# All dense products of a hybrid decoder layer by Strassen's seven block products, with attention and recurrence fed from DRAM

## The chip, the core and the metric

The kernel runs on one core of a Trainium2 chip. Its engines are TensorE (PE: matrix products, with PEld its weight loads), VectorE (DVE), ScalarE (ACT), GpSimd (POOL) and SyncE (SP, which here only issues DMAs). Each works through its own list of instructions in order and waits at semaphores for the others. The metric is the device time of one execution in microseconds (us). TensorE's clock has two levels, 1.2 and 2.4 GHz; the profile gives the granted clock as a share of the higher.

## The reference, cut to what matters

One layer over x of 2048 tokens by 1024 features, all in float32:

```
h = x @ w_in                       # (2048,1024) @ (1024,3328)
hq, hf, hi, hg, aq, ak, av, ag = split(h)   # 512,512,512,512 | 512,128,128,512
f   = lb + (1-lb) * sigmoid(hf);  k_in = 1 - f;  q_h = silu(hq)
o_h = hgrn2_chunk(q_h, k_in, hi, log f)     # 4 heads of 128, state 128x128, chunks
o_h = rmsnorm(o_h) * hg_norm_w * silu(hg)
o_a = sliding_window_attention(rope(aq), rope(ak), av, sinks) * silu(ag)
      # 8 query heads and 2 key/value heads of 64, window 128
out = concat(o_h, o_a) @ w_out     # (2048,1024) @ (1024,1024)
z   = 2**0.25 * x + out
return layernorm(z) * ln_g + ln_b
```

The recurrence is S_t = diag(f_t) S_(t-1) + (1-f_t) i_t^T with output S_t^T q_t.

## The kernel before, in words

Every dense product is made with operands split in two: a rounded part `h` (ACT, line 97) and the remainder `l` (line 98, on DVE, or for two of the four x tiles of a block on POOL). Three matmuls, h·h, h·l and l·h, replace one float32 product. `load_split` (line 87) loads a tile from DRAM by SP and splits it. `project_t` (line 104) makes one 128 x 512 product of a weight tile and 512 tokens: eight K tiles, 24 matmuls of 128x512, lines 110 to 112. `project_n` (line 114) does the same with tokens on the partitions, lines 120 to 122.

Three stages follow one another. Attention goes over two key/value heads `j` and four blocks `b` of 512 tokens: it loads and splits x, projects (`kvp`, `qp`, `gp`), rotates, makes scores `sp`, weights `wt`, and the mix, which goes to DRAM (`sw_spill`, line 329). The recurrence goes over two pairs of heads and the same four blocks, loads x again, projects decay and query (`fp`, `hq`), and per 128 tokens values and gates (`vg`); two chunks of 128 tokens then share small products: scores `ap` (lines 444, 447), transposed keys `kp` (line 454) copied by ACT to `kt` (line 459), state updates `hkv` (line 475), outputs `ho` (lines 488, 492), whose squares ACT sums (line 495). The result goes to `hg_spill` (line 506). The output stage takes 16 tiles of 128 tokens: `prepare` (line 333) loads the mix, transposes half of it (`mp`, line 342) and splits it; 48 matmuls give two halves `po` (lines 537 to 539), DVE adds the residual (`z`, line 540) and the layer norm follows.

The program's text is not the order on an engine: a scheduler of the framework moves each instruction as early as its list allows, and the pools set when a buffer is free again: `mm`, `sc` (three accumulators each), `rawp` (3), `wp` (8), `xp` (7). Sixteen matmuls on zeros (line 128) run while the first loads are under way.

## Time and profile before

| | |
|---|---|
| time, median of 3 runs | 949.61 us (949.59 to 952.05) |
| profiled execution: span | 951.3 us |
| PE busy | 933.0 us (98%) |
| PE weight loads busy | 750.7 us (79%) |
| DVE busy | 607.3 us (64%) |
| ACT busy | 308.4 us (32%) |
| POOL busy | 322.0 us (34%) |
| moved by DMA | 91.03 MB, mean 96 GB/s |

The profiled execution is one run with the profiler on; its span from first to last instruction is 951.3 us, 0.18% above the median of the timed runs. Busy times of matmuls overlap, since one enters the array while the one before drains; the step from one matmul to the next is read from a chain instead.

### The profile page before, as it was taken

What the parts mean: (1) busy time and instruction counts of PE and PEld (TensorE: products, weight loads), DVE (VectorE), ACT (ScalarE), POOL (GpSimd) and SP (SyncE); (2) the same over time, 40 slices, a digit from 0 to 9 for tenths busy, and PEclk for the clock granted to TensorE, in tenths of its full rate; (3) what the DMA queues carried; (4) which work ended last, traced back from release to release, by engine and by line L of the source; (5) the groups of instructions that cost most, each with busy time, mean ns of one, the idle gap of its engine ahead of it and who ended that gap; (6) DMA issues with size and microseconds to landing.
All of it is one profiled execution on the core that took longest, in us unless ns stands there. A gap on an engine that the chain in (4) does not pass through costs nothing.

```text
span 951.3 us, 12917 instructions
## 1 busy us (share of the span) xinstructions
PE 933.0 (98%) x4744; PEld 750.7 (79%) x4744; DVE 607.3 (64%) x1233; ACT 308.4 (32%) x785; POOL 322.0 (34%) x306
## 2 busy tenths in 40 slices
PE   8999999999998999999999999999999989999996
PEld 7878777777786777878887887888788878888885
DVE  5877887867879955726366383726458446666554
ACT  5455545544564423131142423122133211000000
POOL 1645536445447534313042642313133111111111
PEclk9999999999999999999999999999999999999998
DMA  7423243033242403002032321103013253444321
GB/s 261 165 72 123 70 158 124 33 106 106 78 151 94 127 12 101 23 12 100 1 122 78 100 100 65 47 1 102 10 56 123 78 188 134 143 152 146 113 99 57
DMA packets 33216, 91.03 MB, mean 96 GB/s; under 512 B 4224, under 2 KB 12416, under 8 KB 33152
## 3 DMA queue, kind: packets, MB, share of 16 engines
q1 hardware_dynamic: 27792, 73.41, 23.7%
q0 software_dynamic: 2912, 8.40, 2.5%
q10 hardware_dynamic: 2448, 8.39, 2.2%
q8 instruction: 37, 0.61, 0.3%
q14 instruction: 27, 0.22, 0.1%
HBM read 73.41 MB, written 16.78 MB: 95 GB/s over the span
## 4 chain that ended last, share of the span: by engine, by line
PE 85%; DVE 6%; DMA 4%; ACT 3%; issue 1%; SPq 0%; POOL 0%; POOLq 0%; DVEq 0%; ACTq 0%
PE vg L121 6%; PE vg L120 6%; PE vg L122 6%; PE po L537 6%; PE po L539 6%; PE po L538 6%; PE fp L110 3%; PE fp L111 3%; PE fp L112 3%; PE hq L112 3%; PE hq L110 3%; PE hq L111 3%; PE op L320 3%; PE qp L112 2%; PE qp L110 2%; PE qp L111 2%
## 5 line engine op out<-in xcount | busy, mean ns | idle before, releaser
L537 PE MATMUL po<-wo_h,mh 128*128 128x512 f32 (+1 forms) x264 | 103.1, 391 | 2.8 <-DVE z L540 2.8
L539 PE MATMUL po<-wo_h,ml 128*128 128x512 f32 (+1 forms) x264 | 102.0, 386 | 0.0
L538 PE MATMUL po<-wo_l,mh 128*128 128x512 f32 (+1 forms) x264 | 101.9, 386 | 0.0
L120 PE MATMUL vg<-wh_h,xh_h 128*128 128x512 f32 x256 | 100.8, 394 | 0.0
L121 PE MATMUL vg<-wh_l,xh_h 128*128 128x512 f32 x256 | 100.8, 394 | 0.0
L122 PE MATMUL vg<-wh_h,xh_l 128*128 128x512 f32 x256 | 100.7, 394 | 0.0
L98 POOL TENSOR_TENSOR xh_l<-xh_raw,xh_h 128x1024 fp32r<-128x1024 f32 x16 | 39.1, 2448 | 125.6 <-ACT xh_h L97 122.9
L540 DVE SCALAR_TENSOR_TENSOR z<-xr,po 128x512 f32<-128x512 f32 (+1 forms) x33 | 22.1, 672 | 70.3 <-PE po L539 64.3
L545 POOL TENSOR_SCALAR rs<-mv 128x1 f32<-128x1 f32 x16 | 9.4, 584 | 151.4 <-DVE mv L543 151.4
L283 ACT ACTIVATE wt<-sp,st 128x128 f32<-128x128 f32 x128 | 45.8, 365 | 44.4 <-DVE st L279 44.0
L537 PEld LDWEIGHTS po<-wo_h,mh 128*128 128x128 f32 x264 | 50.1, 190 | 12.4 <-DVE z L540 3.0
L293 POOL TENSOR_TENSOR wt<-wt,st 128x512 f32<-128x512 f32 x32 | 37.4, 1169 | 61.9 <-DVE st L292 35.2
L539 PEld LDWEIGHTS po<-wo_h,ml 128*128 128x128 f32 x264 | 50.0, 189 | 10.1
L538 PEld LDWEIGHTS po<-wo_l,mh 128*128 128x128 f32 x264 | 50.0, 189 | 9.5
L343 ACT ACTIVATE mh<-mp 128x512 fp32r<-128x512 f32 x16 | 9.6, 599 | 144.8 <-PE mp L342 144.8
L120 PEld LDWEIGHTS vg<-wh_h,xh_h 128*128 128x128 f32 x256 | 48.4, 189 | 10.1 <-issue 0.6
L121 PEld LDWEIGHTS vg<-wh_l,xh_h 128*128 128x128 f32 x256 | 48.1, 188 | 10.2 <-issue 0.6
L122 PEld LDWEIGHTS vg<-wh_h,xh_l 128*128 128x128 f32 x256 | 48.1, 188 | 9.9 <-issue 0.4
L395 DVE RECIPROCAL re<-e 128x512 f32<-128x512 f32 x16 | 53.5, 3344 | 0.0
L433 DVE SCALAR_TENSOR_TENSOR hg<-tg,vg 128x256 f32<-128x256 f32 x32 | 13.4, 420 | 60.2 <-ACT tg L431 60.2
L110 PE MATMUL fp<-xh_h,wh_h 128*128 128x512 f32 x128 | 51.2, 400 | 0.0
L110 PE MATMUL qp<-xa_h,wa_h 128*128 128x512 f32 x128 | 50.7, 396 | 0.0
(173 smaller groups left out, 2483.9 us busy)
## 6 DMA issues: line engine op xcount, KB each, us to landing
xh_raw<-in_xt_dram SPq DMA_DIRECT2D x32, 512.0 KB, 3.6
xa_raw<-in_xt_dram SPq DMA_DIRECT2D x28, 512.0 KB, 3.7
wh_raw<-in_wt_dram SPq DMA_DIRECT2D x16, 512.0 KB, 3.4
xr<-in_xn_dram SPq DMA_DIRECT2D x16, 512.0 KB, 3.6
out_dram<-y ACTq DMA_DIRECT2D x15, 512.0 KB, 2.6
wa_raw<-in_wt_dram SPq DMA_DIRECT2D x9, 512.0 KB, 4.9
cs<-in_rope_dram SPq DMA_DIRECT2D x8, 512.0 KB, 3.4
sw_spill<-mix POOLq DMA_DIRECT2D x32, 128.0 KB, 2.5
```

Of the source, the lines that this page charges most:

```text
L98: engines[lo_eng].tensor_sub(lo[:, c], raw[:, c], hi[:, c].bitcast(F32))
L110: nc.tensor.matmul(ps, lhsT=wh[:, r], rhs=xh[:, c], start=k == 0, stop=False)
L111: nc.tensor.matmul(ps, lhsT=wh[:, r], rhs=xl[:, c], start=False, stop=False)
L112: nc.tensor.matmul(ps, lhsT=wl[:, r], rhs=xh[:, c], start=False, stop=k == KT - 1)
L120: nc.tensor.matmul(ps, lhsT=xh[:, r], rhs=wh[:, c], start=k == 0, stop=False)
L121: nc.tensor.matmul(ps, lhsT=xh[:, r], rhs=wl[:, c], start=False, stop=False)
L122: nc.tensor.matmul(ps, lhsT=xl[:, r], rhs=wh[:, c], start=False, stop=k == KT - 1)
L283: nc.scalar.activation(wt_[:, s, :], sps[s // 2][:, s % 2, P:], AF.Exp, bias=st[:, 1, s : s + 1], scale=0.125, accum_out=st[:, 3, s : s + 1],)
L395: nc.vector.reciprocal(re, e[:, :, 1:129])
L537: nc.tensor.matmul(ps, lhsT=mh[:, e, :], rhs=wh[:, c], start=e == 0, stop=False)
L538: nc.tensor.matmul(ps, lhsT=mh[:, e, :], rhs=wl[:, c], start=False, stop=False)
L539: nc.tensor.matmul(ps, lhsT=ml[:, e, :], rhs=wh[:, c], start=False, stop=e == 7)
```

## The change

The kernel is written anew around 2 x 2 block products in Strassen's manner (the variant with seven products and shared sums). x is taken in two super-blocks `s` of 1024 tokens. In each, x is cut in halves by tokens and by K into `a11`, `a12`, `a21`, `a22`, and the seven operands `a11`, `a12`, `a22`, `s1` to `s4` are made by DVE, split (`put`), and kept on chip for the super-block, one buffer each. The 26 weight tiles are taken in 13 pairs; the seven combinations of a pair's blocks are made and split (`w_rest`), four of them go to DRAM in the first super-block (`kept_w`) and are loaded again in the second. A product is four K tiles of three matmuls. `Pair` runs the seven into accumulators `px`, `py`, `pz`; ACT takes three snapshots of them, DVE adds three times, and four 128 x 512 projections come out, which `finish` writes to DRAM: queries, keys and values of attention split (`hl`), the rest whole (`proj`). For the first three pairs of a super-block, the products 1 and 2 of all three stand ahead of the others (GROUP).

Attention (`attend`) and recurrence (`recur`) load from DRAM what they need. A table `jobs` says ahead of which pair each of the eight attention and eight recurrence blocks is written; two recurrence blocks come in the output stage. The recurrence loads its values and gates transposed and turns them by PE (128 transposes of 128 x 128, line 540 after). The output product takes pairs of token tiles: seven operands of w_out take the x operands' buffers, and seven of each mixed pair are made by DVE and POOL. Accumulators are six in one pool. The POOL DMA queue's scratch is 4096 bytes.

```diff
-LO_ENGINES = "dpdp"
+PAIRS = [(0, 5), (1, 2), (3, 4), (6, 7), (8, 9)] + [
+    (10 + 8 * j + 2 * i, 11 + 8 * j + 2 * i) for j in range(2) for i in range(4)
+]
+GROUP = 3
...
+    def split2(src, h, l):
+        nc.scalar.activation(h, src, AF.Copy)
+        nc.vector.tensor_sub(l, src, h.bitcast(F32))
+    def w_split(src, name):
+        w = w_tile(name)
+        split2(src, w[:, 0], w[:, 1])
+        return w
+    def put(made, n, q, src, name):
+        h = xc.tile([P, 512], F32R, tag=f"{n}{q}h", name=f"{name}_{n}{q}h")
+        l = xc.tile([P, 512], F32R, tag=f"{n}{q}l", name=f"{name}_{n}{q}l")
+        split2(src, h, l)
+        made[n][q] = (h, l)
...
+    def x_sums(s, made):
+        n = f"x{s}"
+        for q in range(4):
+            a21, a22 = load_x(s, 1, q, f"{n}_p21{q}"), load_x(s, 1, 4 + q, f"{n}_p22{q}")
+            a11 = load_x(s, 0, q, f"{n}_p11{q}")
+            s1, s2 = tmp_tile(f"{n}_s1{q}"), tmp_tile(f"{n}_s2{q}")
+            nc.vector.tensor_add(s1, a21, a22)
+            nc.vector.tensor_sub(s2, s1, a11)
+            put(made, "s2", q, s2, n)
+            put(made, "s1", q, s1, n)
+        for q in range(4):
+            a11, a21 = load_x(s, 0, q, f"{n}_r11{q}"), load_x(s, 1, q, f"{n}_r21{q}")
+            s3 = tmp_tile(f"{n}_s3{q}")
+            nc.vector.tensor_sub(s3, a11, a21)
+            put(made, "s3", q, s3, n)
+        for q in range(4):
+            a12 = load_x(s, 0, 4 + q, f"{n}_r12{q}")
+            s4 = tmp_tile(f"{n}_s4{q}")
+            h, l = made["s2"][q]
+            nc.vector.tensor_sub(s4, a12, h.bitcast(F32))
+            nc.vector.tensor_sub(s4, s4, l.bitcast(F32))
+            put(made, "s4", q, s4, n)
+        for q in range(4):
+            put(made, "a22", q, load_x(s, 1, 4 + q, f"{n}_r22{q}"), n)
...
+    def w_rest(s, pair, w, again):
+        n = f"w{s}_{pair[0]}"
+        if s == 1:
+            for m in (6, 5, 7):
+                w[m] = w_tile(f"{n}_{m}")
+                nc.sync.dma_start(w[m].bitcast(F32), kept_w[pair, m])
+            w[3] = w_split(load_w(s, pair[1], 1, ""), f"{n}_3")
+            w[4] = w_tile(f"{n}_4")
+            nc.sync.dma_start(w[4].bitcast(F32), kept_w[pair, 4])
+            return
+        b11, b21 = load_w(s, pair[0], 0, ""), load_w(s, pair[0], 1, "")
+        b12, b22 = load_w(s, pair[1], 0, ""), load_w(s, pair[1], 1, "")
+        if not again:
+            w[1], w[2] = w_split(b11, f"{n}_1"), w_split(b21, f"{n}_2")
+        def keep(m, t):
+            w[m] = w_split(t, f"{n}_{m}")
+            nc.gpsimd.dma_start(kept_w[pair, m], w[m].bitcast(F32))
+        t1, t2 = tmp_tile(f"{n}_t1"), tmp_tile(f"{n}_t2")
+        nc.vector.tensor_sub(t1, b12, b11)
+        nc.vector.tensor_sub(t2, b22, t1)
+        keep(6, t2)
+        keep(5, t1)
+        nc.vector.tensor_sub(t1, b22, b12)
+        keep(7, t1)
+        w[3] = w_split(b22, f"{n}_3")
+        nc.gpsimd.tensor_sub(t2, b21, t2)
+        keep(4, t2)
...
+    def finish(pair, row, col, s, t):
+        w, b = pair[col], 2 * s + row
+        if w >= 10:
+            nc.gpsimd.dma_start(proj[w][b], t)
+            return
...
+        h, l = t_tile(f"h{w}_{b}", F32R), t_tile(f"l{w}_{b}", F32R)
+        split2(t, h, l)
+        nc.gpsimd.dma_start(hl[j][kind][b][0], h.bitcast(F32))
+        nc.gpsimd.dma_start(hl[j][kind][b][1], l.bitcast(F32))
...
+        def snap(self, ps, what):
+            t = c_tile(f"{what}_{self.n}")
+            with tc.high_priority():
+                nc.scalar.activation(t, ps, AF.Copy)
+            return t
+        def joined(self, row, col, ps, t):
+            with tc.high_priority():
+                nc.vector.tensor_add(t, ps, t)
+            finish(self.pair, row, col, self.s, t)
+        def mul(self, ps, m, n, first):
+            product(ps, tiles_of(self.w[m]), self.x[n], first)
+        def first(self):
+            self.px = mm_ps(f"px{self.n}")
+            self.mul(self.px, 1, "a11", True)
+            self.s1 = self.snap(self.px, "s1")
+        def second(self):
+            py = mm_ps(f"py{self.n}")
+            self.mul(py, 2, "a12", True)
+            self.joined(0, 0, py, self.s1)
+        def rest(self):
+            px = self.px
+            self.mul(px, 6, "s2", False)
+            s2 = self.snap(px, "s2")
+            pz = mm_ps(f"pz{self.n}")
+            self.mul(pz, 5, "s1", True)
+            s5 = self.snap(pz, "s5")
+            self.mul(px, 7, "s3", False)
+            self.joined(1, 1, px, s5)
+            self.mul(pz, 3, "s4", False)
+            self.joined(0, 1, pz, s2)
+            self.mul(px, 4, "a22", False)
+            finish(self.pair, 1, 0, self.s, self.snap(px, "c10"))
...
+    def wo_sums(made):
+        for e in range(4):
+            b11, b12, b22 = load_wo(e, 0, ""), load_wo(e, 1, ""), load_wo(e + 4, 1, "")
+            t1, t2 = tmp_tile(f"wo_t1{e}"), tmp_tile(f"wo_t2{e}")
+            nc.vector.tensor_sub(t1, b12, b11)
+            nc.vector.tensor_sub(t2, b22, t1)
+            put(made, "s2", e, t2, "wo")
+            put(made, "s1", e, t1, "wo")
...
+        w = {1: w_split(a11, f"{n}_1"), 2: w_split(a12, f"{n}_2")}
+        s1, s2 = tmp_tile(f"{n}_s1"), tmp_tile(f"{n}_s2")
+        nc.vector.tensor_add(s1, a21, a22)
+        nc.vector.tensor_sub(s2, s1, a11)
+        w[6] = w_split(s2, f"{n}_6")
+        w[5] = w_split(s1, f"{n}_5")
+        nc.gpsimd.tensor_sub(s1, a11, a21)
+        w[7] = w_split(s1, f"{n}_7")
+        nc.gpsimd.tensor_sub(s2, a12, s2)
+        w[3] = w_split(s2, f"{n}_3")
+        w[4] = w_split(a22, f"{n}_4")
+        return w
...
+    jobs = {
+        (0, 5): [(attend, 0, 0)],
...
+        (1, 3): [(recur, 0, 1)],
+        (1, 5): [(recur, 1, 0)],
+        (1, 6): [(attend, 0, 2)],
...
+    out_jobs = {0: [(recur, 1, 2)], 2: [(recur, 1, 3)]}
+    for s in range(2):
+        group = PAIRS[:GROUP]
+        ws = []
+        for p, pair in enumerate(group):
+            ws.append(w_first(s, pair))
+            if p == 0 and s == 0:
+                x_first(0, x, "a11")
+        if s == 0:
+            x_first(0, x, "a12")
+        x_sums(s, x)
+        ps = [Pair(s, pair, w, x) for pair, w in zip(group, ws)]
+        for p in ps:
+            p.first()
+        for p in ps:
+            p.second()
+        for t, pair in enumerate(PAIRS):
+            if t < GROUP:
+                w_rest(s, pair, ws[t], True)
+            if GROUP - 1 <= t < len(PAIRS) - 1:
+                w_next = prepare_w(s, PAIRS[t + 1])
+            if t == len(PAIRS) - 1:
+                nxt = units()
+                if s == 0:
+                    x_first(1, nxt, "a11")
+                    x_first(1, nxt, "a12")
+                else:
+                    wo_first(nxt)
+            for f, *a in jobs.get((s, t), []):
+                f(*a)
+            if t < GROUP:
+                ps[t].rest()
+            else:
+                p = Pair(s, pair, w, x)
+                p.first()
+                p.second()
+                p.rest()
+            w = w_next if t >= GROUP - 1 else None
+        x = nxt
+    wo_sums(x)
+    m = out_prepare(0)
+    for i in range(T // P // 2):
+        if i + 1 < T // P // 2:
+            m_next = out_prepare(i + 1)
+        for f, *a in out_jobs.get(i, []):
+            f(*a)
+        out_pair(i, m, x)
+        m = m_next
```

In the order of instructions three places matter. The first is DVE near the start of the program. Before, `xa_0_0` is the first block's first K tiles, `l` the remainder of a split, and PE needs only these:

```order
L98 TENSOR_TENSOR wa_0_l<-wa_0_raw,wa_0_h 128x512 [waits DMAHW0_49,Activation_49]
L98 TENSOR_TENSOR wa_0_l<-wa_0_raw,wa_0_h 128x512 [waits DMAHW1_49,Activation_49]
L98 TENSOR_TENSOR xa_0_0_l<-xa_0_0_raw,xa_0_0_h 128x512 [waits DMAHW2_49,Activation_49]
L98 TENSOR_TENSOR xa_0_0_l<-xa_0_0_raw,xa_0_0_h 128x512 [waits DMAHW3_49,Activation_49]
L98 TENSOR_TENSOR xa_0_1_l<-xa_0_1_raw,xa_0_1_h 128x512 [waits DMAHW4_49,Activation_49]
L147 CAST past<-wz 128x128 [waits Pool_49]
L98 TENSOR_TENSOR xa_0_1_l<-xa_0_1_raw,xa_0_1_h 128x512 [waits DMAHW5_49,Activation_49]
```

After, `x_` names the operands of x, `x_s` and `w_0_t` sums, `w_0_6` the sixth combination of the first weight pair; these rows are number 73 to 80 in DVE's list:

```order
L185 TENSOR_TENSOR x_s42l<-x_s_539,x_s42h 128x512 [waits Activation_49]
L245 TENSOR_TENSOR x_s_548<-x_s_548,x_s23l 128x512 [waits DVE_49]
L185 TENSOR_TENSOR x_a222l<-x_r_567,x_a222h 128x512 [waits DMAHW5_49,Activation_49]
L185 TENSOR_TENSOR x_a223l<-x_r_573,x_a223h 128x512 [waits DMAHW7_49,Activation_49]
L185 TENSOR_TENSOR x_s43l<-x_s_548,x_s43h 128x512 [waits Activation_49]
L280 TENSOR_TENSOR w_0_t_700<-w_5_0_696,w_0_0_692 128x512 [waits DMAHW6_49,DMAHW0_49]
L281 TENSOR_TENSOR w_0_t_701<-w_5_1_698,w_0_t_700 128x512 [waits DMAHW1_49,DVE_49]
L185 TENSOR_TENSOR w_0_6_704<-w_0_t_701,w_0_6_704 128x512 [waits Activation_49]
```

On PE the 72 matmuls of products 1 and 2 of three pairs stand ahead of these, and the last three of them are the first rows here:

```order
L332 MATMUL py_3_674<-x_a123h,w_3_2_396 128x512
L333 MATMUL py_3_674<-x_a123l,w_3_2_396 128x512
L334 MATMUL py_3_674<-x_a123h,w_3_2_396 128x512
L332 MATMUL px_0_579<-x_s20h,w_0_6_704 128x512 [waits Activation_49]
L333 MATMUL px_0_579<-x_s20l,w_0_6_704 128x512 [waits DVE_49]
```

Before, PE's first products stand behind one or two splits each; after, its 73rd dense matmul stands behind 66 DVE operations of 128x512.

The second place is PE in the middle of the recurrence. Before, `vg` is a dense product of values, and `ho` an output of the recurrence:

```order
L120 MATMUL vg_2_3_4603<-wh_5_h,xh_2_1_h 128x512
L121 MATMUL vg_2_3_4603<-wh_5_l,xh_2_1_h 128x512
L492 MATMUL ho_2_0_4523<-u_0_2_1_4541,kq_2_4334 128x128 [waits DVE_49]
L488 MATMUL ho_2_0_4523<-hv_2_1_4499,at_3355 128x128
L492 MATMUL ho_2_0_4523<-u_1_2_1_4543,kq_2_4409 128x128 [waits DVE_49]
L122 MATMUL vg_2_3_4603<-wh_5_h,xh_2_1_l 128x512
L120 MATMUL vg_2_3_4603<-wh_6_h,xh_2_2_h 128x512
```

After, the `vg` rows are transposes; `kp` are the transposed keys, which ACT copies to `kt`, and `hkv` the state updates:

```order
L551 MATMUL ap_3_0_7391<-kq_3_7312 64x128
L552 MATMUL ap_3_0_7391<-kq_3_7312 64x64
L555 MATMUL kp_3_0_7392<-ident,kq_3_7312 128x128
L578 MATMUL hkv_3_0_7411<-hv_3_0_7373,kt_3_0_7407 128x128 [waits Activation_49]
L578 MATMUL hkv_3_0_7411<-hv_3_0_7373,kt_3_0_7407 128x128
L578 MATMUL hkv_3_1_7430<-hv_3_0_7373,kt_3_0_7407 128x128 x2
L540 MATMUL vg_3_2_7465<-ident,r_3_7365 128x128
L540 MATMUL vg_3_2_7465<-ident,r_3_7367 128x128
L540 MATMUL vg_3_2_7465<-ident,r_3_7369 128x128
L540 MATMUL vg_3_2_7465<-ident,r_3_7371 128x128
L540 MATMUL vg_3_3_7473<-ident,r_3_7365 128x128 [waits DVE_49]
L540 MATMUL vg_3_3_7473<-ident,r_3_7367 128x128
```

Before, dense matmuls lie between the small ones; after, none does, from the first chunk's transposes to the second chunk's outputs.

The third place is DVE where the output stage begins. Before, `ml` is the remainder of the mixed tokens' split and `z` the residual sum:

```order
L483 TENSOR_TENSOR s_0_3_3_6934<-u_0_3_3_6928,hkv_3_3_6927 128x128 [waits DVE_49,PE_49]
L483 TENSOR_TENSOR s_1_3_3_6936<-u_1_3_3_6930,hkv_3_3_6927 128x128 [waits DVE_49]
L344 TENSOR_TENSOR ml_6990<-mp_6991,mh_6989 128x512 [waits Activation_49]
L346 TENSOR_TENSOR ml_7075<-m_7069,mh_7074 128x512 [waits DMAHW2_49,DMAHW0_49,Activation_49]
L503 SCALAR_TENSOR_TENSOR hmix_3_1_6953<-ho_3_1_6910,rstd_3_1_6950,hg_3_2_6859 128x128 [waits DMASW0_49,Activation_49,Pool_49]
L503 SCALAR_TENSOR_TENSOR hmix_3_1_6953<-ho_3_1_6910,rstd_3_1_6950,hg_3_2_6859 128x128
L503 SCALAR_TENSOR_TENSOR hmix_3_1_6953<-ho_3_1_6910,rstd_3_1_6950,hg_3_3_6890 128x128 x2
L344 TENSOR_TENSOR ml_7075<-mp_7076,mh_7074 128x512 [waits Activation_49]
L346 TENSOR_TENSOR ml_7160<-m_7154,mh_7159 128x512 [waits DMAHW6_49,DMAHW4_49,Activation_49]
L540 SCALAR_TENSOR_TENSOR z_7002<-xr_6976,po_0_7004 128x512 [waits DMASW2_49,DMAHW7_49,DMASW1_49,DVE_49]
```

After, `wo_` are sums and splits of w_out, and `m_1` the first operand of the mixed pair 0, with which PE's first output product begins:

```order
L185 TENSOR_TENSOR wo_s33l<-wo_t_7785,wo_s33h 128x512 [waits Activation_49]
L641 TENSOR_TENSOR wo_t_7797<-wo_t_7797,wo_s20l 128x512 [waits DVE_49]
L641 TENSOR_TENSOR wo_t_7806<-wo_t_7806,wo_s21l 128x512 [waits DVE_49]
L640 TENSOR_TENSOR wo_t_7815<-wo60d,wo_s22h 128x512 [waits DMAHW5_49,DVE_49]
L185 TENSOR_TENSOR wo_a220l<-wo_t_7797,wo_a220h 128x512 [waits Activation_49]
L641 TENSOR_TENSOR wo_t_7815<-wo_t_7815,wo_s22l 128x512 [waits DVE_49]
L185 TENSOR_TENSOR wo_a221l<-wo_t_7806,wo_a221h 128x512 [waits Activation_49]
L640 TENSOR_TENSOR wo_t_7824<-wo70d,wo_s23h 128x512 [waits DMAHW6_49,DVE_49]
L185 TENSOR_TENSOR m_1_7855<-mh_7831,m_1_7855 128x512 [waits DMAHW7_49,DMAHW0_49,Activation_49]
L185 TENSOR_TENSOR m_2_7858<-ms_7832,m_2_7858 128x512 [waits DMAHW2_49,DMAHW1_49,Activation_49]
```

Before, w_out was loaded and split during the recurrence and the first mixed tile stood among the last state updates; after, about 65 rows of w_out's sums and splits and of recurrence (1, 2) stand ahead of the first mixed pair's first split.

## Rows read from the trace of the kernel before

**Rows 1.** The page, busy time, share of the span and count by engine:

```profile
PE 933.0 (98%) x4744; PEld 750.7 (79%) x4744; DVE 607.3 (64%) x1233; ACT 308.4 (32%) x785; POOL 322.0 (34%) x306
```

**Rows 2.** The page, chain that ended last, share of the span:

```profile
PE 85%; DVE 6%; DMA 4%; ACT 3%; issue 1%; SPq 0%; POOL 0%; POOLq 0%; DVEq 0%; ACTq 0%
```

**Rows 3.** Windows; the first line names the columns:

```profile
core 0: us, PE busy (x) PEld busy (x) DVE busy (x) ACT busy (x) POOL busy (x), PEclk, DMA share, GB/s
0.00:50.00 50.00, 47.21 (x211) 39.11 (x212) 35.69 (x64) 27.00 (x44) 20.00 (x24) 0.97 0.62 210
300.00:350.00 50.00, 46.72 (x236) 35.46 (x235) 43.33 (x90) 21.35 (x65) 28.71 (x28) 0.97 0.29 90
400.00:450.00 50.00, 50.00 (x264) 40.39 (x263) 23.27 (x51) 12.86 (x34) 12.63 (x13) 1.00 0.16 53
750.00:800.00 50.00, 47.20 (x230) 38.25 (x229) 27.22 (x54) 7.95 (x20) 8.85 (x12) 0.97 0.51 165
900.00:951.00 51.00, 43.19 (x217) 36.52 (x215) 28.20 (x47) 1.72 (x3) 8.05 (x10) 0.95 0.22 81
```

**Rows 4.** The chain of waits by line, 800 to 900 us:

```profile
by line: PE po L537 32.2%; PE po L539 32.2%; PE po L538 32.0%; PE mp L342 3.9%
```

**Rows 5.** Groups by line, 800 to 900 us: busy us, mean ns, idle before:

```profile
L537 PE MATMUL po<-wo_h,mh 128*128 128x512 f32 x141 | 55.8, 396 | 0.0
L342 PE MATMUL mp<-ident,m 128*128 128x128 f32 x36 | 5.4, 271 | 0.0
```

**Rows 6.** Groups by line, whole span, last its releaser:

```profile
L395 DVE RECIPROCAL re<-e 128x512 f32<-128x512 f32 x16 | 53.5, 3344 | 0.0
L98 DVE TENSOR_TENSOR xh_l<-xh_raw,xh_h 128x1024 fp32r<-128x1024 f32 x16 | 25.8, 1613 | 15.0 <-ACT xh_h L97 14.8
L98 POOL TENSOR_TENSOR wh_l<-wh_raw,wh_h 128x1024 fp32r<-128x1024 f32 x8 | 19.6, 2449 | 0.1
L346 DVE TENSOR_TENSOR ml<-m,mh 128x512 fp32r<-128x512 f32 x16 | 10.4, 650 | 0.0
L98 DVE TENSOR_TENSOR wh_l<-wh_raw,wh_h 128x1024 fp32r<-128x1024 f32 x8 | 10.2, 1276 | 4.4 <-ACT wh_h L97 4.4
L98 DVE TENSOR_TENSOR wo_l<-wo_raw,wo_h 128x1024 fp32r<-128x1024 f32 x8 | 10.1, 1279 | 3.6 <-ACT wo_h L97 3.6
```

**Rows 7.** Timeline of the start: start us, duration, engine, line, instruction, [wait]:

```profile
8.28 0.69 DVE L98 TENSOR_TENSOR xa_l<-xa_raw,xa_h 128x512 fp32r<-128x512 f32 x1 [2.15 <-ACT xa_h L97]
8.30 0.49 PE L110 MATMUL kvp<-xa_h,wa_h 128*128 128x512 f32 x1 [0.55 <-ACT xa_h L97]
10.64 1.29 DVE L98 TENSOR_TENSOR xa_l<-xa_raw,xa_h 128x512 fp32r<-128x512 f32 x2 [1.66 <-ACT xa_h L97]
```

**Rows 8.** Short windows at the start and after 780 us, columns as in Rows 3:

```profile
10.00:12.00 2.00, 1.34 (x3) 0.81 (x4) 1.36 (x4) 1.81 (x3) 0.00 (x0) 0.61 1.05 403
14.00:16.00 2.00, 2.00 (x10) 1.65 (x9) 2.00 (x4) 1.89 (x4) 0.00 (x0) 1.00 1.02 406
780.00:782.00 2.00, 2.00 (x6) 1.52 (x6) 2.00 (x5) 0.00 (x0) 0.82 (x2) 0.54 0.86 313
```

**Rows 9.** Timeline at the output stage's start:

```profile
777.38 0.50 PE L537 MATMUL po<-wo_h,mh 128*128 128x512 f32 x1 [2.80 <-DVE z L540]
```

**Rows 10.** Groups by line, PE's small products of the recurrence:

```profile
L488 PE MATMUL ho<-hv,at 128*128 128x128 f32 x128 | 24.4, 275 | 0.0
L475 PE MATMUL hkv<-hv,kt 128*128 128x128 f32 x128 | 18.8, 274 | 0.0
```

**Rows 11.** Groups by line, ACT in the recurrence:

```profile
L495 ACT ACTIVATE junk<-ho 128x128 f32<-128x128 f32 x64 | 17.7, 277 | 40.3 <-PE ho L492 39.0
L495 ACT ACTIVATION_READ_ACCUMULATOR junk<-ho 128x1 f32 x64 | 12.6, 197 | 0.0
L459 ACT ACTIVATE kt<-kp 128x512 f32<-128x512 f32 x16 | 9.5, 592 | 14.9 <-PE kp L454 14.9
```

**Rows 12.** The page, DMA traffic:

```profile
DMA packets 33216, 91.03 MB, mean 96 GB/s; under 512 B 4224, under 2 KB 12416, under 8 KB 33152
```

879 lines of the change are left out of this document (454 added, 425 removed).

## Prediction, made before the changed kernel ran

> **What bounds the kernel now.** I read the page's totals first: TensorE (PE) is busy for 933.0 of 951.3 us, the VectorE (DVE) for 64%, the ScalarE (ACT) for 32%, GpSimd (POOL) for 34% [rows 1]. Then the chain of waits: 85% of it is PE, 6% DVE, 4% DMA [rows 2]. So PE sets the time, nearly alone. Third, the windows: a full stretch has PE busy for all of its 50 us, and only four lose much: the first (47.2), the one where attention gives way to the recurrence (46.7), the one where the output stage starts (47.2), and the end [rows 3]. Last, the pitch of a dense product. A busy time of a matmul overlaps the next one, so I take the chain in an undisturbed stretch: 32.2% of 100 us for the 141 matmuls of line 537 is 0.228 us each, and 3.9 us for 36 transposes of 128x128 is 0.108 us [rows 4, 5]. Before has 3264 dense matmuls of 512 columns (two of 256 counted as one): 744 us of the 951.
>
> **What the change takes from PE.** Two by two blocks go through seven products instead of eight. Projections: 13 pairs of weight tiles, 2 super-blocks, 7 products of 12 matmuls = 2184 where 2496 were; output: 8 pairs of token tiles, 84 each = 672 where 768 were. That is 408 matmuls fewer, 408 x 0.228 = **-93 us**. The recurrence's values and gates now come out transposed, so 128 transposes of 128x128 come in: 128 x 0.108 = +14. Other small matmuls stay as they were, less about 1. PE's own work falls by **80 us**. If PE stayed busy throughout, that would be the whole answer.
>
> **What it puts on the others.** Each combination of x, of w_in and of w_out must be summed and split into a rounded part (ACT) and a remainder (DVE). In the changed program 294 such splits, 99 sums and 134 additions out of the accumulators stand, nearly all 128x512. A split's remainder took DVE 0.650 us, 1.279 for twice the columns [rows 6]. On DVE 294 x 0.65 + 99 x 0.65 + 134 x 0.67 = 345 us come in; its old remainders, residual sums, rotations and norms, about 220, go: 607 becomes about 733 us. Reckoned the same way ACT goes from 308 to about 540 (splits, 104 snapshots, the scalings that move to it), POOL from 322 to about 390. None exceeds PE's remaining work. So no engine becomes the bound on average; the question is where PE arrives before its operands. Four places follow.
>
> **1. The start.** Before, the first product of real data began at 8.30 us, and the first eight K slices fed PE from then on [rows 7]. Now PE has the products 1 and 2 of three pairs, 72 matmuls x 0.228 = 16.4 us, and then its next row multiplies `s2` by `w_0_6`, whose remainder is DVE's row 80 in program order. Ahead of it stand 66 DVE operations of 128x512 and 14 small ones: all of the x sums of the first super-block. Data comes slowly at first (by 11.9 us before had done four of them [rows 7]); 63 x 0.67 + 2 from there is 55 us. PE has then done 8.3 + 16.4 = 24.7 us: it waits some 30 us, where before lost one or two. **+29**. The cover would be other PE work in that time, and there is none in its order. The loads can't be faster than that either: 12 MB stand in SP's queue up to the last of these weights, at 403 to 406 GB/s [rows 8] 30 us, and SP's queue also holds four loads of attention's keys, which wait for the first projections to be written, ahead of the weights that `w_0_6` is made of. Bounds: 20, if DVE's sums run at 0.5 us; 36, if those loads are late.
>
> **2. The second super-block.** The x units have one buffer each. While the last pair of the first super-block runs, `s2`, `s1`, `s3`, `s4`, `a22` can't be replaced. From the last use of `s2` on PE has 48 + 72 matmuls, 27 us; in that time stand 40 sums and splits and some ten joins on DVE, 33 us, and 15.7 MB of x, weights and kept combinations on the queues, 39 us at the 403 GB/s of [rows 8]. **+12** (6 to 20). Before's own loss at its stage change, about 3.3 us in [rows 3], goes.
>
> **3. The output.** The seven w_out units take the x units' buffers. Between the last product on them and the first output product stand about 65 DVE rows in order: 20 splits, 20 sums, the decay and gates of recurrence (1, 2) with two reciprocals of 3.34 us [rows 6], and then the split of the first mixed tile; 42 us, and PE has the rest of the pair and this recurrence, about 19 us. That is 22 us of waiting, and the next two token pairs, whose seven operands each are made by the same DVE, wait another 11 to 14. **+35**, less the 2.8 us that before waited there for an accumulator, and the slow matmuls behind it (clock 0.54) [rows 8, 9], 5 in all: **+30** (15 to 45).
>
> **4. The recurrences.** Before, dense products of the values lie between the recurrence's small ones; PE never stood in front of `hkv` or `ho` (idle 0.0) [rows 10]. Now the projections are done, and in PE's order seven clumps of 54 to 72 small matmuls have no dense one among them. In each half `hkv` waits for the transposed keys (0.592 on ACT), which wait for the transposes, and the second half's `hkv` stands behind the first half's on ACT: four squares of 0.474 with their accumulator reads, four scalings, keys [rows 11], about 4.5 us a clump. Seven would be 31 us; nothing, where ACT runs ahead since PE is late elsewhere. I take 22.
>
> Two small terms: the tail, where six operations follow the last product (+2), and the clock. It fell to 0.54 behind before's wait of 2.8 us [rows 8, 9], so PE's four long waits now cost perhaps +5 together.
>
> **Sum**: -80 + 29 + (12 - 3) + 30 + 22 + 7 = +17 on the profiled execution's 951.3 us: 968. That execution stands 0.18% above the median of the runs, so 966 us.
>
> **A rule weighed.** What speaks against the change is in [rows 6]: DVE's remainders took 1.276 us for `wh_l` but 1.613 for `xh_l`, both 128x1024 with two SBUF inputs; GpSimd ran the same operation at times, in 2.449 against some half of that. The Trainium skill, "SBUF — State Buffer", section "SBUF: two separate sides", says that a DVE operation with two SBUF inputs and a GpSimd operation that reads SBUF exclude each other for the whole instruction. By the row a slowed operation costs 26%; by the rule it would cost up to the other's full length. The sum above uses the undisturbed 0.65.
>
> **Rivals.**
> A. *PE stays the bound.* DVE and ACT run ahead whenever PE is busy, and the DVE work of 733 us fits under PE's 824. For it: every stretch of [rows 3] has DVE at 0.47 to 0.93 of PE's busy time, so there is slack to run ahead, and the order places sums of the next pair before the products of this one. Against it: the x and w_out units with one buffer, and the start, where there is nothing to run ahead of. With 10 at the start, 5 at each change and 5 in the recurrences, less the old losses of 8: 951 - 80 + 17 = 888; the extremes are 871 and 940. The Trainium skill, "Perfetto Trace Analysis", section "Identifying the Most-Contended Engine", would have the engine with most occupancy improved first, and judges PE by weight loads, 79% here; by that rule the whole cut should arrive, which is this rival.
> B. *DVE pays for GpSimd.* At 1.613/1.276 the terms 1 to 3, which are DVE's lists, grow by 26% of their 130 us: +34, so 1000. It decides from about half of DVE's pairs disturbed (+17, 983). For it: 272 DMA issues of GpSimd where 51 were, and 56 additions of 256 columns there in the output stage. Against it: GpSimd's big remainders, the likely partners, are gone.
> C. *DMA.* By the order's sizes 214 MB move where 91.03 did [rows 12]: kept combinations 27.3 written and read again, projections 21 both ways. At 403 GB/s this is 530 us of transfer, 55% of the span, no bound on average; but a kept combination that lands late in the second super-block stops PE for each pair. Four us for each of 13 pairs: 951 - 80 + 29 + 52 + 30 + 22 = 1004.
>
> **Chances.** The forecast 0.50, with a range of its own from 940 to 1000: its four terms are each uncertain by a third or more, and the recurrences may cost nothing. A 0.33, B 0.10, C 0.07. The range of 8 in 10: below 897 lies a third or so of A (0.11), above 1012 parts of B and C (0.08). A measurement of this kernel tells 0.3% from nothing: 947 to 952. Faster: A, and one tenth of the forecast's half, 0.38. Same 0.06. Slower 0.56.
>
> **What would show it.** Pitch of a dense matmul 0.23 us and 2856 of them (step 1's -93). PE idle between about 25 and 55 us, released by the DVE remainder of `w_0_6`. Two stretches of low PE busy near the middle and 150 to 200 us before the end, released by x and w_out units and by the first `m` splits on DVE. PE idle before `hkv` of 2 us or so, released by ACT's `kt`. PE busy falls to about 87% of the span; under rival A it stays over 95%. DVE remainders of 128x512 near 0.82 instead of 0.65 would show B; waits of PE or DVE on DMA in the second super-block, C. The forecast is wrong if PE's waits at the four places sum to less than 60 us.

## The result

The changed kernel takes 1181.03 us (median of 4 runs, 1174.49 to 1189.1) where the kernel before takes 950.83: the ratio is 1.242, with a 95% interval from 1.237 to 1.248. The sign was forecast, the size was not: 966 us, with a range to 1012.

The page of the profile after, busy time by engine, answers to [rows 1]:

```profile
PE 926.5 (79%) x4446; PEld 721.9 (61%) x4446; DVE 711.2 (60%) x1339; ACT 484.4 (41%) x1236; POOL 399.7 (34%) x587
```

No engine is full: PE fell from 98% of the span to 79%, and DVE, ACT and POOL came out near the sums of the forecast (733, 540, 390). So the time is lost in waits. The windows, columns as in [rows 3], show where:

```profile
0.00:50.00 50.00, 22.57 (x104) 18.84 (x104) 38.64 (x74) 24.07 (x40) 10.29 (x25) 0.79 0.79 242
50.00:100.00 50.00, 37.09 (x152) 29.93 (x153) 36.72 (x53) 17.06 (x30) 20.47 (x29) 0.87 0.79 265
250.00:300.00 50.00, 49.06 (x246) 38.12 (x245) 29.81 (x61) 21.68 (x67) 17.28 (x27) 1.00 0.53 190
400.00:450.00 50.00, 34.22 (x124) 25.52 (x123) 36.02 (x58) 16.58 (x29) 10.45 (x13) 0.76 0.84 300
450.00:500.00 50.00, 32.49 (x163) 26.03 (x162) 27.56 (x51) 18.05 (x34) 16.94 (x26) 0.80 0.60 205
550.00:600.00 50.00, 34.32 (x179) 27.31 (x180) 24.34 (x48) 19.27 (x55) 13.27 (x20) 0.76 0.43 128
750.00:800.00 50.00, 32.70 (x186) 24.45 (x186) 25.29 (x54) 17.93 (x52) 15.83 (x26) 0.76 0.35 116
900.00:950.00 50.00, 15.69 (x67) 10.58 (x65) 42.60 (x74) 27.17 (x49) 10.79 (x11) 0.63 0.62 207
1050.00:1100.00 50.00, 50.00 (x238) 41.61 (x237) 36.58 (x60) 19.01 (x39) 27.21 (x33) 1.00 0.42 139
```

The reader is to see that a stretch without a stage change or a recurrence block (250 to 300, 1050 to 1100) is as full as before's, and that 400 to 450 is the second super-block, 900 to 950 the output's start, and 450, 550 and 750 a recurrence block each. In those the granted clock (the column before the last two) falls too, to 0.76 to 0.80.

Added up over windows of 2 us, each with its PE busy time and granted clock, the span divides in three: time in which PE did nothing; time that PE's busy windows lost at the lower of its two levels, 1.2 GHz (busy times one less the granted clock); and the rest, its work at 2.4 GHz.

| | before | after | change |
|---|---|---|---|
| PE idle, us | 18.3 | 253.3 | +235.0 |
| lost to the lower clock, us | 4.8 | 61.9 | +57.1 |
| work, us | 928.2 | 864.6 | -63.6 |
| span, us | 951.3 | 1179.8 | +228.5 |

Which waits make the 253.3? PE's own list (who waits, for whom: us in all, times, the longest), its seven largest:

```profile
PE kp L555 <- POOL kq L522: 81.1, 11, 13.8
PE px L332 <- ACT w L184: 36.4, 3, 32.9
PE mp L656 <- DMA mh<-hg_spill: 26.2, 9, 7.7
PE hkv L578 <- ACT kt L560: 15.5, 11, 2.3
PE ox L332 <- DVE xr L700: 10.2, 2, 9.3
PE pz L332 <- ACT w L184: 9.8, 1, 9.8
PE vg L540 <- DMA r<-proj: 9.6, 2, 9.1
```

The largest is not one that I had priced: PE stands in front of the first transposed keys `kp` of each recurrence block, and GpSimd's decayed keys `kq` release it. One block's chain, from the timeline of the changed kernel (start, duration, engine, line, instruction, [wait]):

```profile
466.30 5.76 SPq L265 DMA_DIRECT2D w<-kw  x3
...
472.15 13.63 SPq L497 DMA_DIRECT2D r<-proj  x8
...
477.85 0.63 ACT L508 ACTIVATE r<-r 128x512 f32<-128x512 f32 x1 [4.85 <-DMA r<-proj]
478.51 0.81 ACT L510 ACTIVATE f<-r,c,c 128x512 f32<-128x512 f32 x1
479.36 0.29 DVE L516 TENSOR_TENSOR_SCAN e<-f 128x64 f32<-128x64 f32 x1 [5.63 <-ACT f L510]
...
480.95 3.35 DVE L519 RECIPROCAL f<-e 128x512 f32<-128x512 f32 x1
...
484.39 1.04 POOL L522 TENSOR_TENSOR kq<-r,f 128x256 f32<-128x256 f32 x1 [2.19 <-DVE f L519]
...
485.48 0.48 PE L555 MATMUL kp<-ident,kq 128*128 128x128 f32 x1 [13.78 <-POOL kq L522]
```

PE had finished its pair at 485.48 - 13.78 = 471.70. The first loads of the block's projections (`r`) were issued at 472.15: they stand in SP's list behind three loads of kept weights, which wait until PE releases a weight buffer, so they can't come before PE is nearly done with the pair. SP's own list of waits has this for line 265, the kept weights' (of its other releasers the next is `pz`, 24.5 us):

```profile
SPq L265 <- PE px L334: 53.2, 20, 5.2
```

Then it is one thing after another: 5.7 us to landing, 1.5 on ACT, 1.6 of scans, 3.35 of a reciprocal, 1.04 on GpSimd. DVE itself stood idle for 5.63 us of it.

### The profile page after: what moved, and what is told of

Its sections match the earlier page's. It is cut to its first block, busy times and chain, and to the rows that moved or that the text cites. A ratio compares the mean times of both kernels' runs of the same rounds, so it can differ in the third digit from the quotient of the medians.

```text
span 1179.8 us, 14699 instructions
## 1 busy us (share of the span) xinstructions
PE 926.5 (79%) x4446; PEld 721.9 (61%) x4446; DVE 711.2 (60%) x1339; ACT 484.4 (41%) x1236; POOL 399.7 (34%) x587
## 2 busy tenths in 40 slices
DMA packets 98079, 215.11 MB, mean 182 GB/s; under 512 B 14160, under 2 KB 24016, under 8 KB 98000
## 5 line engine op out<-in xcount | busy, mean ns | idle before, releaser
L555 PE MATMUL kp<-ident,kq 128*128 128x128 f32 x64 | 21.3, 384 | 82.6 <-POOL kq L522 81.1
L185 DVE TENSOR_TENSOR w<-w,w 128x512 fp32r<-128x512 f32 x46 | 32.6, 709 | 51.6 <-ACT w L184 48.7
L722 POOL TENSOR_TENSOR xr<-xr,lb 128x256 f32<-128x256 f32 x56 | 53.5, 984 | 22.3 <-DVE xr L718 20.1
L575 POOL TENSOR_SCALAR ue<-u,e 128x128 f32<-128x128 f32 x60 | 38.2, 645 | 63.4 <-ACT u L573 63.3
L184 ACT ACTIVATE w<-w_t 128x512 fp32r<-128x512 f32 x52 | 32.6, 629 | 53.6 <-PE py L334 13.0
L519 DVE RECIPROCAL f<-e 128x512 f32<-128x512 f32 x16 | 53.5, 3344 | 0.2
L349 ACT ACTIVATE s<-px 128x512 f32<-128x512 f32 x52 | 31.0, 596 | 53.4 <-PE px L334 50.8
L185 DVE TENSOR_TENSOR w<-w_t,w 128x512 fp32r<-128x512 f32 x52 | 43.6, 842 | 9.5 <-ACT w L184 9.2
L450 ACT ACTIVATE wt<-sp,st 128x129 f32<-128x129 f32 x128 | 45.4, 375 | 3.4 <-DVE st L446 3.4
L436 PE MATMUL sp<-kh,qa 128*128 128x256 f32 (+1 forms) x128 | 34.6, 300 | 7.4 <-DMA qa<-hl 5.4
L578 PE MATMUL hkv<-hv,kt 128*128 128x128 f32 x128 | 27.6, 383 | 15.5 <-ACT kt L560 15.5
L551 PE MATMUL ap<-kq 128*64 128x128 f32 x128 | 31.3, 359 | 9.9 <-DVE kq L529 6.0
```

Of the source, the lines that this page charges most:

```text
L184: nc.scalar.activation(h, src, AF.Copy)
L185: nc.vector.tensor_sub(l, src, h.bitcast(F32))
L436: nc.tensor.matmul(sp[:, h, lo:], lhsT=lhs, rhs=kh[:, kc], start=True, stop=False)
L450: nc.scalar.activation(wt_[:, s, :], sps[s // 2][:, s % 2, P - 1 :], AF.Exp, bias=st[:, 1, s : s + 1], scale=0.125, accum_out=st[:, 2, s : ...
L519: nc.vector.reciprocal(re, e[:, :, 1:129])
L551: nc.tensor.matmul(ap_[0:64, s, :], lhsT=kn[h][:, c, 0:64], rhs=qn[h][:, c, :], start=True, stop=True)
```

## The experiments

My theory after this: the recurrence's operands are made too late by a serial chain that starts in SP's queue, PE's order puts the block's products ahead of dense ones that could run, and each of PE's stops costs slow clock behind it; start, second super-block and output are the forecast's own terms. The rivals: the vector engines or the DMA are simply too slow for the new work everywhere, or DVE and GpSimd slow one another.

**The chain started one pair earlier (e1_ahead).** The function `recur` is cut in two: `prep` has the loads of decays and queries, gates, scans, reciprocals and `kq`, the new `recur` the loads of values and gates and the products.

```diff
-    def recur(j, b):
+    def prep(j, b):
...
+    def recur(j, b):
...
+        (1, 2): [(prep, 0, 1)],
         (1, 3): [(recur, 0, 1)],
...
```

> The recurrence block is cut in two: its loads, gates, scans, reciprocals and decayed keys and queries are written one pair ahead of its products, everything else as in the changed kernel. Theory (PE stands in front of the transposes of the keys because loads, scans, reciprocals and GpSimd's product start only when PE is nearly there; some 100 us of PE's idle time in eight blocks, and slow clock behind each): the idle time ahead of these transposes falls from 81 us to under 25, the loss to the lower clock from 62 us to about 40, the time from 1181 to 1050 to 1090. Rival (the vector engines are late everywhere, so what is made earlier makes something else late): the waits come back as waits on weight and x operands, the time stays over 1150.

Measured 1153.82 us (1151.33 to 1156.38): 27 less than the changed kernel, not 90 to 130. PE's waits ahead of `kp` fell from 81.1 to 53.6 us only. Of the five first waits in the second super-block two fell by 8.7 and 10.5 us, two by 1.6 and 2.8, and one, at 633 us, not at all (10.80 before, 10.81 here). Its timeline says why (same columns):

```profile
611.93 9.35 SPq L265 DMA_DIRECT2D w<-kw  x3
...
621.32 0.43 SPq L499 DMA_DIRECT2D r<-proj  x1
...
633.58 0.47 PE L566 MATMUL kp<-ident,kq 128*128 128x128 f32 x1 [10.81 <-POOL kq L524]
```

Writing the loads earlier didn't move them past the kept weights: they still left SP only when the last of those had got its buffer. Neither theory nor rival had that. The time lies where the rival had put it, over 1150, but the edit did too little to tell the two apart.

**The reciprocals left out (e2_norecip).**

```diff
-            nc.vector.reciprocal(re, e[:, :, 1:129])
+            nc.vector.tensor_copy(re, e[:, :, 1:129])
```

> The changed kernel with the 16 reciprocals of the decays replaced by copies of the same size (the output isn't the reference's). Theory (the chain behind a block's loads is serial): each block's first wait shrinks by the reciprocal's 3.34 us less a copy's 0.5, the second by up to as much: 4 to 5 us in eight blocks, 30 to 45 us in all with the clock. Rival (the loads of the recurrence alone decide, or the vector engine's queue): under 15 us.

Measured 1152.93 us (1147.95, 1157.91): 28 less, just under what was expected, with 10 us between the two runs. The copy took 0.84 us on the mean instead of 3.34, 40 us less DVE time in all 16. The first waits of the five blocks in the second super-block fell by 10 us together (59.1 to 49.0), but all waits ahead of `kp` by 5.8 only (81.1 to 75.3), since later ones grew; those of `hkv` for `kt` fell by 9.9 (15.5 to 5.6). The reciprocal is one link of the chain and not the whole of it; the loads still came when they came.

**The recurrence's loads on GpSimd's queue (e3_rpool).**

```diff
-            nc.sync.dma_start(t, proj[w][b])
+            nc.gpsimd.dma_start(t, proj[w][b])
```

> The changed kernel with the recurrence's loads from DRAM issued by GpSimd instead of SP. In the changed kernel's trace they stand in SP's queue behind loads of kept weights that wait for a weight buffer. Theory: they start 3 to 8 us earlier per block, the time falls by 20 to 60 us. Rival (they wait for their own buffers, which the projections' staging shares, in whatever queue): within 10 us of 1181, or slower, since GpSimd's spills stand behind them.

Measured 1207.79 us: 27 more, as the rival had it. The waits ahead of `kp` fell a little, to 69.3 us, but PE now waited 49.6 us in front of the value transposes `vg` for these loads (9.6 before): in GpSimd's list these loads stand behind spills and behind the products `kq` of their own block.

**A larger first group (e4_group4).**

```diff
-GROUP = 3
+GROUP = 4
```

> GROUP 4 instead of 3: 24 more matmuls of products 1 and 2 stand ahead of the first product that needs an x sum, in both super-blocks. Theory (PE's first wait of 33 us is DVE's list of sums, which nothing else covers): the wait falls by about 5.5 us less the 1.4 us that the fourth pair's two weight splits add to DVE, and about the same at the second super-block: 1170 to 1178. Rival (the loads of the first weights end it): no change at the start.

Measured 1179.20 us (1173.71, 1184.70), no difference that two runs could tell. The first wait fell from 32.95 to 27.02 us, somewhat more than expected, but PE stopped for 2.68 us within the group, and longer in the second super-block (11.8 us in front of `pz` where it was 9.8): what was gained at the start was given back.

**Dense products ahead of the recurrence's (e5_later).** To e1_ahead's cut comes another place for the products; the preparation of block (1, 2), which e1_ahead had written ahead of the last pair, goes back to the output stage.

```diff
             for f, *a in jobs.get((s, t), []):
-                f(*a)
+                if f is not recur:
+                    f(*a)
+            if t >= GROUP:
+                p = Pair(s, pair, w, x)
+                p.first()
+                p.second()
+            for f, *a in jobs.get((s, t), []):
+                if f is recur:
+                    f(*a)
             if t < GROUP:
                 ps[t].rest()
             else:
-                p = Pair(s, pair, w, x)
-                p.first()
-                p.second()
                 p.rest()
```

> As the run with the recurrence cut in two, and now its products are also written behind products 1 and 2 of their pair, so that 24 to 66 dense matmuls (5 to 15 us) come ahead of each block's first transposes in TensorE's order. The loads stand in SP's queue as before. Theory (the chain from loads to decayed keys is serial and ends 8 to 14 us after the pair boundary): dense work now covers it, the wait ahead of the transposes falls from 81 us to under 20, the time to 1060 to 1110. Rival (what PE does earlier it lacks later: it is short of operands in every stage): the waits move to the dense products, and the time stays within 20 us of 1154.

Measured 1134.74 us (1129.59 to 1138.98): 46 less than the changed kernel, 19 less than e1_ahead. From PE's list of waits in this run:

```profile
PE vg L551 <- DMA r<-proj: 32.6, 10, 15.0
PE mp L667 <- DMA mh<-hg_spill: 17.3, 8, 5.8
PE kp L566 <- POOL kq L524: 12.0, 5, 4.7
```

The wait for `kq` went from 81.1 (53.6 in e1_ahead) to 12.0 us, as the theory said: dense products cover the chain. A part came back as the theory did not say: 32.6 us in front of the values' transposes, whose four loads are the last of the block in SP's queue, 14.5 in front of attention's queries (5.4 in the changed kernel) and 15.0 of dense products in front of ACT's snapshots (6.4). So the time fell by about half of what was expected, and 19 us from e1_ahead is just within the 20 that the rival allowed: the theory was right on the wait, and the rival in part on what it is worth.

**The output's start (e6_both, e10_outlater).** On top of e5_later, first the mixed pair 0 ahead of w_out's sums, then also the two late recurrence blocks behind the products of a token pair (the second one's preparation moves with it, from token pair 1 to 2):

```diff
-    out_jobs = {0: [(prep, 1, 2), (recur, 1, 2)], 1: [(prep, 1, 3)], 2: [(recur, 1, 3)]}
+    out_jobs = {0: [(prep, 1, 2), (recur, 1, 2)], 2: [(prep, 1, 3), (recur, 1, 3)]}
...
+    m = out_prepare(0)
     wo_sums(x)
-    m = out_prepare(0)
...
+        out_pair(i, m, x)
         for f, *a in out_jobs.get(i, []):
             f(*a)
-        out_pair(i, m, x)
```

> The run before this one, with the first mixed token pair loaded and split ahead of the sums of w_out instead of behind them. Theory (at the output's start the mixed tiles' loads stand behind 32 loads of w_out in SP's queue, and their splits behind 40 operations of DVE): the 26 us that PE waits for them go, 10 to 25 us less than the run before. Rival (the w_out operands are late then, since each has one buffer): within 8 us of it.

> The run with the first mixed pair ahead of w_out's sums, and the two recurrence blocks of the output stage written behind the products of token pairs 0 and 2 instead of ahead of them. Theory (the output starts late because DVE and SP work through a recurrence block and w_out at once): of the 56 us that PE stands idle from 850 to 1000 us 15 to 30 go, 1126 becomes 1095 to 1112. Rival (w_out's own 40 operations and 32 loads are enough to hold it): within 8 us of 1126.

The first gave 1126.51 us (1123.76 to 1128.58), 8 less than e5_later, short of the 10 to 25 expected and at the edge of the rival's 8: one wait of 19.58 us for the mixed tiles' load took the place of several, and from 850 to 1000 us PE's idle time even rose, from 52.7 in e5_later to 62.4 us. What fell is the loss to the lower clock, from 69 to 57 us in the whole span. The second gave 1099.64 us (1098.72 to 1102.59), 27 less again; that is the fastest of all variants, 1.156 times the kernel before (1.153 to 1.159). Its windows at the output's start:

```profile
850.00:900.00 50.00, 34.20 (x147) 24.31 (x146) 45.06 (x77) 29.39 (x61) 11.47 (x14) 0.79 0.68 229
900.00:950.00 50.00, 47.14 (x220) 37.01 (x219) 42.45 (x77) 27.71 (x71) 32.92 (x39) 0.87 0.39 129
```

From 850 to 1000 us PE now stands idle for 26.2 us, where e6_both had 62.4 and the changed kernel 56.9 (the 56 of the text above); 15.8 of them are the stage change, in the first of these windows. What was in the way was a recurrence block and w_out going through DVE and SP at once.

**GpSimd's subtractions on DVE (e7_nopool)**, three lines, 29 operations:

```diff
-        nc.gpsimd.tensor_sub(t2, b21, t2)
+        nc.vector.tensor_sub(t2, b21, t2)
```

> The changed kernel with the three subtractions of weights and mixed tokens that GpSimd makes (29 in all) on DVE. Theory (VectorE's remainders of 0.84 and 0.87 us where 0.65 is undisturbed are slowed by these operations of GpSimd): the two groups fall to about 0.70, and the time changes by less than 15 us, since DVE sets the end in the start and the output alone. Rival (contention between the two engines is the main loss): 40 us or more less.

Measured 1165.67 us (1163.67, 1167.67), 15 less. The remainders in question, of the changed kernel and then of this run (count, busy us, mean ns):

```profile
L185 DVE TENSOR_TENSOR w<-w_t,w 128x512 fp32r<-128x512 f32 x52 | 43.6, 842 | 9.5 <-ACT w L184 9.2
L185 DVE TENSOR_TENSOR m<-m_s,m 128x512 fp32r<-128x512 f32 x32 | 27.7, 870 | 3.3 <-ACT m L184 3.2
```

```profile
L185 DVE TENSOR_TENSOR w<-w_t,w 128x512 fp32r<-128x512 f32 x52 | 37.5, 722 | 8.4 <-ACT w L184 8.3
L185 DVE TENSOR_TENSOR m<-m_s,m 128x512 fp32r<-128x512 f32 x32 | 24.3, 769 | 0.9 <-ACT m L184 0.7
```

The contention is there, 842 against 722 ns, but in these 29 operations it is worth some 15 us of 230: rival B falls as the main cause. GpSimd's other operations stayed, so this doesn't price all of it.

**Kept weights on another queue (e8_kwpool).**

```diff
-                nc.sync.dma_start(w[m].bitcast(F32), kept_w[pair, m])
+                nc.gpsimd.dma_start(w[m].bitcast(F32), kept_w[pair, m])
...
```

> The changed kernel with the kept weights of the second super-block loaded by GpSimd's queue, so that SP's queue doesn't wait for weight buffers ahead of the recurrence's loads. Theory: the loads of the five blocks in the second super-block start 3 to 9 us earlier, PE's waits ahead of the transposes fall there by as much, 15 to 40 us in all, less what GpSimd's own waits for weight buffers hold up. Rival (the loads wait for their own staging buffers): under 10 us, or slower.

Measured 1166.68 us (1165.38, 1167.99), 14 less, just under the 15 to 40 expected and over the rival's 10. The same block as above, from this run's timeline up to 482 us, six of the eight loads:

```profile
473.54 8.24 SPq L497 DMA_DIRECT2D r<-proj  x6
...
488.23 0.48 PE L555 MATMUL kp<-ident,kq 128*128 128x128 f32 x1 [8.82 <-POOL kq L522]
```

PE's wait began at 488.23 - 8.82 = 479.41, so the loads now left 5.9 us ahead of it, where they left 0.45 us behind it; the wait fell from 13.78 to 8.82. In the five blocks of the second super-block the first wait fell from 59.1 us together (13.78, 12.81, 10.80, 10.97, 10.72) to 38.0. This shows the first link: SP's queue held these loads up behind weights that waited for buffers. Of these 21 us the run as a whole kept 14; in front of attention's queries a wait for their load grew from 3.70 to 7.19 us.

**The x sums left out (e9_nosums)** in the first super-block; loads, splits and matmuls stay:

```diff
-            s1, s2 = tmp_tile(f"{n}_s1{q}"), tmp_tile(f"{n}_s2{q}")
-            nc.vector.tensor_add(s1, a21, a22)
-            nc.vector.tensor_sub(s2, s1, a11)
+            s1, s2 = a21, a22
...
```

> The changed kernel with the 20 sums of x left out in the first super-block: s1 to s4 are made of the loaded blocks as they are (the output isn't the reference's); loads, splits and matmuls stay. Theory (PE's first wait of 33 us is DVE's list of 66 operations): 46 are left, the wait falls by 20 x 0.65 = 13 us to about 20. Rival (12 MB of loads or SP's queue with attention's loads in it decide): the wait stays over 28 us.

Measured 1163.55 us (1162.54, 1164.55), 17 less. PE's first wait:

```profile
52.07 0.79 PE L338 MATMUL px<-x_s20h,w 128*128 128x512 f32 x1 [23.04 <-ACT w L184]
```

It fell by 9.9 us, from 32.95, for 13 us of sums; 3.1 of these are PE's, which came to the wait later, so the operand was ready 6.8 us earlier (52.07 against 58.83). DVE was done with the x operands 10.5 us earlier (42.04 against 52.56) and then stood longer for a weight's load. In SP's queue this load stands behind attention's keys, and here SP waited 3.6 us for those; in the changed kernel the load got its buffer only from DVE's last x remainder. Here, and there:

```profile
48.29 0.69 DVE L286 TENSOR_TENSOR w_t<-w,w 128x512 f32<-128x512 f32 x1 [6.25 <-DMA w<-in_wt_dram]
```

```profile
56.14 0.69 DVE L280 TENSOR_TENSOR w_t<-w,w 128x512 f32<-128x512 f32 x1 [3.57 <-DMA w<-in_wt_dram]
```

So DVE's list is most of what PE waits for at the start, and attention's keys in SP's queue stand right behind it. The other 7 us that this run gained are not accounted for.

**All of it (e11_all):** e10_outlater with the edits of e7_nopool and e8_kwpool.

> The run before this one with the two smaller edits that each took 14 us alone: GpSimd's subtractions on DVE, and the kept weights loaded by GpSimd's queue. If the gains add: 28 us less than it, 1070 to 1090. If PE's waits are covered by one another: 10 us or less. It doesn't reach the kernel before: start, second super-block and lower clock alone stand for 33 + 20 + 50 us, and the attention's and output's waits stay.

Measured 1105.13 us (1101.05 to 1105.66), no gain over 1099.64: two edits that gave 15 and 14 us alone give nothing on top. For e8_kwpool's the reason is at hand: the wait ahead of `kp` that it shortens, 81.1 us in the changed kernel, was down to 14.7 in e10_outlater. For e7_nopool's no run shows one. No variant came near the kernel before.

## Why the prediction was wrong

Its parts, against what was measured:

| step | forecast, us | measured, us |
|---|---|---|
| PE's own work | -80 | -64 |
| start | +29 | first wait 32.95; idle in the first 100 us 40.3, 3.1 before: +37 |
| second super-block | +12, less 3 | idle from 400 to 450 15.8; one wait of 9.76 and five short ones |
| output | +30 | idle from 900 to 1050 58.4 in all, two recurrence blocks among it |
| recurrences | +22 | 81.1 + 15.5 in front of `kp` and `hkv`, besides shorter waits |
| clock | +5 | +57 |

**The start was right**, in mechanism and nearly in size: the last x sum's remainder ended at 52.6 us where I had put the list's end at 55, PE waited for `w_0_6` as said, and e9_nosums shows the list as most of the cause. The line of it:

```profile
58.83 0.80 PE L332 MATMUL px<-x_s20h,w 128*128 128x512 f32 x1 [32.95 <-ACT w L184]
```

The wait was 4 us longer than the sum had it, by a weight's load (3.57 us) that came behind that remainder; late loads I had named as the upper bound.

**The second super-block was right**, in its place and nearly in size, but its long wait did not end at an x unit, as I had said it would. It ended at the split of a weight, whose load left SP behind seven loads of x. The last two lines are SP's longest waits from 414 to 434 us:

```profile
416.75 10.84 SPq L208 DMA_DIRECT2D x_r<-in_xt_dram  x7
430.76 1.53 SPq L253 DMA_DIRECT2D w<-in_wt_dram  x2
434.04 0.80 PE L332 MATMUL pz<-x_s40h,w 128*128 128x512 f32 x1 [9.76 <-ACT w L184]
SPq L208 <- DVE x_s L238: 6.1, 3, 3.4
SPq L253 <- DVE x_s L244: 3.1, 1, 3.1
```

So SP stood there because DVE's sums had not freed the buffers for these loads: of the term's limits it was DVE's list, but it reached PE through a load that needed a buffer, not through an x unit. Three of the five short waits, 2.4 us together, ended at x units.

**The output's term** was right in its place and too small. DVE's list there was as I had put it: it came to the first mixed split at 939.09 us, behind some 40 us of w_out and recurrence. But none of PE's long waits from 900 to 1050 us ended at such a split, the sign that I had named. Of the 58.4 us, 24.5 ended at loads of mixed tiles, 9.05 at loads of the recurrence, and 9.34 at DVE's residual sum of the first token pair. The mixed tiles' loads left SP from 932.26 us on, behind all of w_out's, and they too waited for buffers, first from DVE's sums of w_out, then from GpSimd's of the mixed tokens (one wait of 6.0 us). These loads were not in the term.

**The recurrence's term failed.** The step was "I take 22", from a wait of `hkv` for ACT's transposed keys, 4.5 us a clump, and nothing for the block's first matmul. That wait came (15.5 us, 11 times, up to 2.3). But I had read the clumps in PE's order only from their first transposes on. Ahead of them stands the chain of loads, gates, scans, two reciprocals and GpSimd's product, and I had asked of it only whether DVE's sum of work fits under PE's, not when its first link could start. The links were within my reach: 3.344 us for a reciprocal [rows 6], and 3.4 to 4.9 us from issue to landing for the largest loads on the page before. [rows 10] had said that `hkv` and `ho` never waited before; the reason, dense products of `vg` beside the chain, I named, and did not price its loss for the chain. The run e5_later shows the price: with the chain written a pair earlier the wait for `kq` fell from 81.1 to 53.6 us, and with the pair's dense products 1 and 2 put ahead as well to 12.0.

**The clock's term failed by its count.** I took +5 for four long waits, from one stop in [rows 8, 9]. Before has 4 stretches of low clock; after has 24, behind short stops too. Of PE's 49 stops of over 1 us 38 stand in such a stretch or have one right behind them; 11 have none, the longest of them 2.48 us. One with a stretch, the wait that ended at 117.43 us after 2.70 us, and the window behind it:

```profile
117.43 0.65 PE L332 MATMUL px<-x_s20h,w 128*128 128x512 f32 x1 [2.70 <-ACT s L349]
```

```profile
118.00:120.00 2.00, 2.00 (x6) 1.52 (x5) 0.97 (x2) 0.93 (x2) 0.00 (x0) 0.50 0.96 277
```

Six matmuls in 2 us, where [rows 8] had ten at the full clock. But for the last, at the end, each stretch cost from 1.2 to 5.3 us; together they are the 61.9.

**PE's work** fell by 64 us, not by 80. The dense pitch stayed: from 1050 to 1100 the chain gives 93.5% of 50 us to 206 dense matmuls, 0.227 us each, and their count is as said. So the 16 us are elsewhere, perhaps in the small products: `kp` for one takes 384 ns on the mean where it took 322, but a part of that is the lower clock, which the table counts by itself. In all eleven variants this rest lies between 859 and 866 us. Whether it is the small products' standing alone or short waits that the profile counts as busy, no run here settles.

**The rivals.** A (the waits hide) is refuted: PE is busy for 79%. B (DVE pays for GpSimd) was real and small, 15 us for the 29 operations tried; its sign, remainders near 0.82, did come (0.842 and 0.870). My reading of [rows 6] was wrong there: 1.613 is not a slowing of every operation by 26%, for in the trace before ten of these sixteen took 1.16 to 1.31 us and six 2.15 to 2.58. C (DMA) fell in the form that I gave it: PE waited for a kept weight to land once, for 1.7 us. But these loads did harm in another way, as a plug in SP's queue.

Two fixes gained less than the wait that they removed (e5_later 46 of 69 us, e8_kwpool 14 of 21), since other waits grew. From the changed kernel to e10_outlater idle time fell by 79 us (253.3 to 174.3) and the time by 81; the slow clock, 61.9 and 61.7, did not move. PE's stops of over 1 us became fewer, 37 where there were 49, but the stretches of low clock did not (23 and 24). Of the 174.3 left, 40 are the start, 18 the second super-block, 16 the output's start, 11 the end, and the rest, about 89, mostly short stops of attention and recurrence that no run here removed. That remainder, with the clock, is more than the 64 us that the seven products save.

## What to carry to other kernels

A cut of an engine's work counts only where its operands are ready: follow each operand that the new order needs back to its first load, and ask in which queue this load stands, what waits ahead of it there and who frees its buffer, before summing busy times. Work that is taken off the bounding engine was also the cover of the chains beside it; when it goes, price the longest of those chains once per block, not only the links that were waited for before. And price the clock behind TensorE's stops, not only their length: most of the longer ones cost slow clock on top, here 62 us beside 253 of waiting.
